# A hybrid decoder step: the prompt's recurrence in four 64-token chunks, laid two to a partition span

## The chip, the cores and the metric

The kernel runs on one core of a Trainium2 chip. The metric is the device time in microseconds (us) of one execution; the median of three runs is used. Engines are named as in the profile: PE is the tensor engine, DVE the vector engine, ACT the scalar engine, POOL GpSimd, SP the engine whose queue issues the DMAs.

## The reference

One layer of a hybrid decoder for a prompt of 256 tokens and 8 sequences of 8 new tokens each ("the sample", 64 tokens), width 2048. A combined input projection feeds a convolution group (31 taps) and an RWKV-7 group of 16 heads of 64; then come an output projection, cross-attention into 256 memory tokens and a gated ConvFFN. The change is in the RWKV-7 group, whose core is this recurrence over the tokens, per head, with a 64x64 state `S`:

```
def wkv_step(S, inp):
    r, w, k, v, a, b = inp
    sa = jnp.einsum('bhij,bhj->bhi', S, a)
    S = S * w[:, :, None, :] + sa[..., None] * b[:, :, None, :] + v[..., None] * k[:, :, None, :]
    y = jnp.einsum('bhij,bhj->bhi', S, r)
    return S, y
...
seq = tuple(jnp.moveaxis(z, 1, 0) for z in (rh, heads(decay), kh, vh, -kk, kk * ah))
S_new, ys = lax.scan(wkv_step, wkv.astype(f32), seq)
```

The prompt starts from a zero state, each sample sequence from its own given state; the states after the last token are outputs too.

## The kernel before

Weights stream from HBM in pieces of 1024 columns in three buffers (`wpiece`, L144 on): ACT writes the upper fp16 part `whi` (L153), DVE the rest `wlo` (L154), and each product of a weight tile takes three fp16 matmuls of 320 columns (`acc`, L56). Everything else is in fp32; in the trace each fp32 matmul stands as two records, a transpose and an fp16 matmul as one.

The order of PE is written out by hand. `drive` takes the weights' matmuls in groups of three, and between them `step` runs a piece of another stream whenever its time has come. A stream is a generator that yields how long its next piece should stay away, in us of a clock that `mm` and `turn` advance by the matmuls' columns. Streams are: `first_stage` (`prepare`, per pair of heads), two `second_stage` streams (`pair`, for the even and the odd pairs), the convolution's taps on DVE (`taps`, `cvmix`, L827 and L829) and its smaller pieces. So one piece of a stream stands on PE as a short run of fp32 matmuls, here called a burst, between the `acc` matmuls. There are 8 pairs of heads; a pair's 128 channels fill the partitions, 64 per head.

`prepare` makes the decayed operands of a pair: `AR` (removal key and receptance), `bt`, `kt`, their token-major copies `tvkb` (`tv`, `tk`, `tb`), and `pc`, the decay over a chunk. `pair` cuts the prompt into two chunks of 128 tokens and does this:

- Score products (`pA`): per chunk and head `bt` and `kt` (64 channels) times `AR`, 128x256 each; DVE masks them into `AB` (L610) and `AM` (L611). The sample has one 64x64 form of them (`AMs`, L618).
- `invert`: the inverse of a triangular 128x128 matrix for 2 chunks x 2 heads by doubling: levels 1 to 4 with 32-row blocks side by side (`psZ`, `psX`), level 5 on 32-blocks, level 6 on 64-blocks (`psZ<-TQ,AB`, `psG<-GG,zm`).
- `sample_state`: the sample's states are loaded as block-diagonal matrices `BD`, one per sequence, transposed (`pS`, 8 per pair) and multiplied with the operands (`pXR`). The decays are spread over the partitions by two fp16 matmuls (`pPC`), and DVE multiplies them with the states into `SD` (L658).
- `prompt_part`: per chunk `solve` makes `pX` (its result `x` copied by ACT), `pU` (`u`, copied by DVE, L684) and `pY`; then the state (`pSc`; `S`, L705, L721 and L722). All of these use the whole 128-row array.
- `sample_part`: its own small `invert`, `solve`, and the new states `pSn`, to which DVE adds `SD` (L754).

PE executes in this fixed order: a burst whose operand is late holds everything behind it.

Of the kernel before, what the change touches and what calls it, by code (L numbers as in the profile page):

```python
# [17 lines left out]
P = 128  # L18
# [27 lines left out]
def hybrid_step_kernel(ctx: ExitStack, tc: tile.TileContext, I, O):  # L46
# [34 lines left out]
    bones16 = cst.tile([P, P], F16, name="bones16")  # L81
    V.tensor_copy(bones16, bones)
# [6 lines left out]
    mask4 = cst.tile([P, 4, P], U8, name="mask4")  # L89
# [4 lines left out]
    RM = cst.tile([P, 330], F16, name="RM")  # L94
    V.memset(RM, 1.0)
    V.memset(RM[:, 0:258:129], 0.0)
    V.memset(RM[:, 258:330:9], 0.0)

# [3 lines left out]
    with tc.tile_pool(name="mk", bufs=1) as mk:  # L102
        f = mk.tile([P, P], F32, name="mkf")
        for ty in range(2):
            G.memset(f, 1.0)
            keep(f, [[1, P]], -1 + ty, -1)
            for z in (ty, ty + 2):
                V.tensor_copy(mask4[:, z, :], f)
# [202 lines left out]
    AMs_ = [ra.tile([P, 3, 4, P], F32, name=f"AM{q}") for q in range(2)]  # L311
    AMss_ = [ra.tile([64, 4, 2, 64], F32, name=f"AMs{q}") for q in range(2)]
    ABs_ = [ra.tile([P, 4, P], F32, name=f"AB{q}") for q in range(2)]
    BDs_ = [ra.tile([P, NB, P], F32, name=f"BD{q}") for q in range(1)]
    LGs_ = ra.tile([P, 330], F32, name="LG")
    GGp_ = [ra.tile([P, 4, P], F32, name=f"GG{q}") for q in range(2)]
    GGs_ = [ra.tile([64, 2, 64], F32, name=f"GGs{q}") for q in range(2)]
    ARS_ = [ra.tile([P, NB, 32], F32, name=f"ARS{q}") for q in range(2)]
    TQ_ = [ra.tile([64, 4, 64], F32, name=f"TQ{q}") for q in range(2)]
    cleared = AMs_ + AMss_  # L320
    for t_ in ABs_ + AMs_ + AMss_ + BDs_ + GGp_ + GGs_ + TQ_ + ARS_:
        (V if any(t_ is v_ for v_ in cleared) else G).memset(t_, 0.0)
# [23 lines left out]
    # d[256+9b+j] pairs pb[256+9b+j] with pb[257+9b+j]; token j of batch b sits at pb[257+9b+1+j]  # L346
# [19 lines left out]
    def invert(A_, GG, TQ, nm, C, nlev):  # L366
# [3 lines left out]
        blk = [slice(32 * q, 32 * q + 32) for q in range(nb)]  # L370
        Gc = rb.tile([C, nm, 32], F32, tag="Gc" + s, name="Gc")
# [3 lines left out]
        for q, r in enumerate(blk):  # L375
            V.copy_predicated(Gc[r, :, 1::2], EM[r, 16 * q:16 * q + 16].unsqueeze(1).broadcast_to([32, nm, 16]), A_[r, :, 32 * q + 1:32 * q + 32:2])
        V.transpose(Tf, Gf)
        yield 1.69
        for lev in range(1, min(nlev, 5)):
# [6 lines left out]
            for a in range(nm):  # L386
                for q, r in enumerate(blk):
                    mm(psZ[r, a * 16:(a + 1) * 16].rearrange("p (n m) -> p n m", m=m), A_[r, a, r], half(Tc, a, r), True, True, True)
# [11 lines left out]
        for q, r in enumerate(blk):  # L400
            (A.copy if q % 2 else G.tensor_copy)(GG[r, :, r], Gc[r])
        if nlev > 5:
            for r in blk[:2]:
                A.copy(TQ[r, :, r], Tc[r])
        for lev in range(5, nlev):
            m = 1 << lev
            first = [slice(2 * q * m, (2 * q + 1) * m) for q in range(C // (2 * m))]
            second = [slice((2 * q + 1) * m, (2 * q + 2) * m) for q in range(C // (2 * m))]
            Tl, Gl = ((lambda r, a: Tc[r, a, :]), (lambda r, a: Gc[r, a, :])) if m == 32 else ((lambda r, a: TQ[r, a, r]), (lambda r, a: GG[r, a, r]))
            psZ = mtile("psZ")  # L410
            for a in range(nm):
                for r1, r2 in zip(first, second):
                    mm(psZ[r2, a * m:(a + 1) * m], A_[r1, a, r2], Tl(r1, a), True, True, True)
            zm = rb.tile([C, nm * 64], F32, tag="zm" + s, name="zm")
            for q, r2 in enumerate(second):
                (V.tensor_copy if q else A.copy)(zm[r2, 0:nm * m], psZ[r2, 0:nm * m])
            yield 3.14
            psG = mtile("psG")
            for a in range(nm):
                for r1, r2 in zip(first, second):  # L420
                    if lev < nlev - 1 and r2.stop <= 64:
                        mm(psG[r2, a * m:(a + 1) * m], Gl(r2, a), zm[r2, a * m:(a + 1) * m], True, True, True)
                    mm(psG[r1, a * m:(a + 1) * m], zm[r2, a * m:(a + 1) * m], Gl(r2, a), True, True, True)
            pv = psG[:, 0:nm * m].rearrange("p (a m) -> p a m", m=m)
            for q, (r1, r2) in enumerate(zip(first, second)):
                if lev < nlev - 1 and r2.stop <= 64:
                    A.copy(TQ[r2, :, r1], pv[r2])
                (V.tensor_copy if q else A.copy)(GG[r1, :, r2], pv[r1])
# [45 lines left out]
    def pr(t_):  # L474
        return t_[:, 0:256].rearrange("p (c t) -> p c t", t=P)
# [10 lines left out]
    def prepare(i, r, k, v):  # L486
        c = slice(i, i + 1)
        # decay, a, gate from the low-rank projections
# [5 lines left out]
        def e_(name, w=T):  # L494
            return ra.tile([P, 330], F32, tag="e", bufs=5, name=name)[:, :w]
# [5 lines left out]
        A.activation(LGs_[:, 0:258].rearrange("p (c t) -> p c t", t=129)[:, :, 1:129], pr(pw), AF.Tanh, bias=hv[:, 0, c], scale=0.5)  # L501
        A.activation(LGs_[:, 258:330].rearrange("p (b e) -> p b e", e=9)[:, :, 1:9], sm(pw), AF.Tanh, bias=hv[:, 0, c], scale=0.5)
# [15 lines left out]
        # inclusive sums of log decay over each chunk  # L518
        L1 = e_("L1", 330)
        V.tensor_scalar(L1, LGs_, 1.0, None, ALU.add)  # L520
        V.tensor_tensor_scan(L1, RM, L1, 0.0, ALU.mult, ALU.add)
        LP = L1[:, 0:258].rearrange("p (c t) -> p c t", t=129)
        LS = L1[:, 258:330].rearrange("p (b e) -> p b e", e=9)
        mid = rb.tile([P, 2, 2], F32, tag="mid", name="mid")
        V.tensor_scalar(mid[:, 0, :], LP[:, :, 64], C1, None, ALU.mult)
        V.tensor_scalar(mid[:, 1, :], LP[:, :, 64], -C1, None, ALU.mult)
        PX = e_("PX", 330)
        PP = PX[:, 0:258].rearrange("p (c t) -> p c t", t=129)
        PS = PX[:, 258:330].rearrange("p (b e) -> p b e", e=9)
        IP = e_("IP")  # L530
        em = rb.tile([P, 2], F32, tag="em", name="em")
        pc = rb.tile([P, 10], F32, tag="pc", bufs=3, name="pc")
        for ch in range(2):
            A.activation(PP[:, ch, :], LP[:, ch, :], AF.Exp, bias=mid[:, 1, ch:ch + 1], scale=C1)
            A.activation(IP[:, ch * P:(ch + 1) * P], LP[:, ch, 1:129], AF.Exp, bias=mid[:, 0, ch:ch + 1], scale=-C1)
        A.activation(PS, LS, AF.Exp, scale=C1)
        A.activation(sm(IP), LS[:, :, 1:9], AF.Exp, scale=-C1)
        A.activation(em, mid[:, 0, :], AF.Exp)
# [1109 lines left out]
```

## Time and profile before

| what | value |
|---|---|
| timed runs | 2122.68, 2119.32, 2120.03 us; median 2120.03 us |
| the profiled execution | 2122.2 us from its first to its last instruction |
| PE busy | 2040.3 us (96%) |
| DVE busy | 1453.0 us (68%) |
| ACT busy | 982.1 us (46%) |
| POOL busy | 582.3 us (27%) |
| stage with the RWKV pairs | about 100 to 650 us of the span |

PE's records overlap, since matmuls are pipelined: a record's own duration is its latency. What a matmul costs PE is read in the time line from its start to the start of the next.

### The profile page before, as it was taken

Reading aid. Unit: us, or ns where it says so; the run is one execution under the profiler, and the core shown is the slowest. Engines: PE = TensorE matmul, PEld = TensorE weight load, DVE = VectorE, ACT = ScalarE, POOL = GpSimd, SP = SyncE. Lnnn points to the kernel's source line nnn. Section 1 sums busy time; section 2 is a strip of 40 time slices with the busy share of each in tenths; the row PEclk is TensorE's granted clock in tenths of the full one; section 3 lists DMA queues with packets and bytes.
Section 4 is the critical chain, followed back from the end, with each engine's and each line's share of the span. In section 5 each row is a group of like instructions: output and inputs, shape, how many; then the busy total and the mean of one; then the engine's idle time right before and its main releaser. Section 6 shows DMA issues by size and latency. Waiting matters only on the chain.

```text
span 2122.2 us, 43823 instructions
## 1 busy us (share of the span) xinstructions
PE 2040.3 (96%) x17221; PEld 1424.2 (67%) x17221; DVE 1453.0 (68%) x2772; ACT 982.1 (46%) x1686; POOL 582.3 (27%) x913
## 2 busy tenths in 40 slices
PE   8999999999899999989999989999999999999998
PEld 6766667576554467566667767777777777777776
DVE  6698798797985834967784497666666666443344
ACT  5434434334544643755673354444444444533332
POOL 4624525335210301210001143433333323000000
PEclk9999999899999999999999999999999999999999
DMA  7533233333246675757784535555555555445444
GB/s 182 159 91 99 73 103 89 82 107 81 91 155 203 216 238 167 244 186 250 246 268 142 169 105 168 161 165 162 159 163 166 159 160 164 141 158 164 156 147 140
DMA packets 301995, 333.26 MB, mean 157 GB/s; under 512 B 33882, under 2 KB 227237, under 8 KB 301764
## 3 DMA queue, kind: packets, MB, share of 16 engines
q1 hardware_dynamic: 301788, 330.46, 51.0%
q8 instruction: 135, 2.21, 0.4%
q14 instruction: 72, 0.59, 0.1%
HBM read 319.90 MB, written 11.22 MB: 156 GB/s over the span
## 4 chain that ended last, share of the span: by engine, by line
PE 74%; DVE 13%; DMA 6%; ACT 2%; issue 2%; POOL 1%; SPq 0%; DVEq 0%; POOLq 0%; ACTq 0%
PE acc L56 58%; PE acck L56 6%; DVE cvmix L829 3%; DVE wlo L154 3%; DMA rawkv<-in_cache_mem_v_dram 2%; PE pA L56 1%; PE pk L60 1%; PE pY L56 1%; DVE vl L1267 1%; DMA out_dram<-fo 1%; ACT whi L153 1%; DMA raw<-in_w_v_dram 1%; ACT vh L1266 1%; PE pos L56 1%; DVE xr L1148 1%
## 5 line engine op out<-in xcount | busy, mean ns | idle before, releaser
L56 PE MATMUL acc<-h,whi 128*128 128x320 f16 (+1 forms) x4736 | 981.3, 301 | 11.5 <-DVE h L1150 3.9
L154 DVE SCALAR_TENSOR_TENSOR wlo<-raw,whi 128x1024 f16<-128x1024 f32 (+1 forms) x512 | 631.3, 1235 | 462.4 <-ACT whi L153 453.6
L56 PEld LDWEIGHTS <-whi 128*128 128x128 f16 (+1 forms) x7080 | 685.9, 99 | 280.5 <-issue 21.8
L153 ACT ACTIVATE whi<-raw 128x1024 f16<-128x1024 f32 (+1 forms) x512 | 533.1, 1044 | 616.3 <-PE acc L56 517.8
L56 PE MATMUL acc<-h,wlo 128*128 128x320 f16 (+1 forms) x2368 | 702.2, 301 | 0.2 <-DVE wlo L154 0.2
L56 PEld LDWEIGHTS <-wlo 128*128 128x128 f16 (+1 forms) x3540 | 348.2, 98 | 142.9 <-issue 7.6
L56 PE MATMUL acc<-act,whi 128*128 128x320 f16 x1320 | 270.3, 299 | 0.0
L56 PE MATMUL acc<-act,wlo 128*128 128x320 f16 x660 | 196.4, 299 | 0.0
L829 DVE SCALAR_TENSOR_TENSOR cvmix<-GB,cdw,cvmix 128x256 f32<-128x256 f32 (+1 forms) x480 | 187.3, 428 | 0.9
L56 PE MATMUL acck<-whi,memo 128*128 128x512 f16 x512 | 151.4, 380 | 0.6 <-ACT memo L949 0.6
L1497 POOL COPY nF<-U 128x9 f32<-128x9 f32 x88 | 52.2, 593 | 307.7 <-DVE U L1496 299.3
L56 PEld LDWEIGHTS <-memo 128*128 128x128 f16 x768 | 73.2, 99 | 80.7 <-issue 2.0
L1494 POOL COPY U<-stF 128x16 f32<-128x16 f32 x88 | 124.5, 1420 | 0.9 <-ACT stF L1482 0.9
L1132 POOL TENSOR_TENSOR sums<-sums,bsq 128x320 f32<-128x320 f32 x33 | 37.9, 1147 | 241.3 <-ACT bsq L1126 239.7
L56 PE MATMUL acck<-wlo,memo 128*128 128x512 f16 x256 | 95.6, 379 | 1.5 <-DVE wlo L154 1.5
L1502 DVE SCALAR_TENSOR_TENSOR C<-U,fdw,C 128x336 f32<-128x336 f32 x176 | 91.3, 558 | 0.1
L1500 ACT ACTIVATE C<-U,fdw 128x336 f32<-128x336 f32 x88 | 55.8, 659 | 31.2 <-DVE U L1496 31.2
L1495 DVE TENSOR_TENSOR U<-acc,rs 128x256 f32<-128x256 f32 x88 | 36.8, 418 | 39.4 <-PE acc L56 39.3
L1267 DVE SCALAR_TENSOR_TENSOR vl<-rawkv,vh 128x1024 f16<-128x1024 f32 x31 | 37.2, 1223 | 31.9 <-ACT vh L1266 31.9
L56 PE MATMUL acc<-oopb,whi 128*128 128x320 f16 x256 | 53.7, 299 | 1.1 <-DVE oopb L190 1.0
L1218 POOL CAST qs<-qf 128x64 f16<-128x64 f32 x16 | 10.0, 626 | 162.5 <-ACT qf L1215 162.5
L56 PE MATMUL acc<-cvmix,whi 128*128 128x320 f16 x256 | 52.1, 299 | 1.5 <-ACT memo L949 1.5
(477 smaller groups left out, 2601.2 us busy)
## 6 DMA issues: line engine op xcount, KB each, us to landing
raw<-in_w_up_dram SPq DMA_DIRECT2D x352, 256.0 KB
raw<-in_w_down_dram SPq DMA_DIRECT2D x71, 512.0 KB
raw<-in_w_in_dram SPq DMA_DIRECT2D x52, 512.0 KB
raw<-in_w_in_dram SPq DMA_DIRECT2D x64, 256.0 KB
raw<-in_w_k_dram SPq DMA_DIRECT2D x32, 512.0 KB
raw<-in_w_v_dram SPq DMA_DIRECT2D x32, 512.0 KB
raw<-in_w_out_dram SPq DMA_DIRECT2D x32, 512.0 KB
rawkv<-in_cache_mem_k_dram SPq DMA_DIRECT2D x32, 512.0 KB
```

Of the source, the lines that this page charges most:

```text
L56: pe[0] = TE.matmul(out, lhsT=lhsT, rhs=rhs, start=start, stop=stop, skip_group_check=skip)
L60: pe[0] = TE.transpose(out, in_, idn)
L153: A.activation(hi[:, :n], raw[:, :n], AF.Copy, scale=SW)
L154: V.scalar_tensor_tensor(lo[:, :n], raw[:, :n], SW, hi[:, :n], ALU.mult, ALU.subtract)
L829: late(V.scalar_tensor_tensor(o_, i_(j), cdw[:, c, j:j + 1], o_, ALU.mult, ALU.add))
L1132: (V if f > 11 else G).tensor_tensor(ssum, ssum, sq, ALU.add)
L1267: V.scalar_tensor_tensor(vl, raw, SX, vh, ALU.mult, ALU.subtract)
L1494: G.tensor_copy(us[:, :, 0:2], stF[:, :, :, j])
L1495: V.tensor_tensor(U[:, 2:258], acc[:, 0:256], rf[:, 0:256], ALU.mult)
L1497: G.tensor_copy(nF[:, :, 0, j], U[:, 256:338:10])
L1500: A.activation(c, U[:, 0:336], AF.Identity, bias=fdw[:, 3, j:j + 1], scale=fdw[:, 0, j:j + 1])
L1502: V.scalar_tensor_tensor(c, U[:, t_:t_ + 336], fdw[:, t_, j:j + 1], c, ALU.mult, ALU.add)
```

## The change

The prompt is cut into four chunks of 64 tokens. Two neighbouring chunks share the partitions: the even one in 0 to 63, the odd one in 64 to 127 (`hcs`). A chunk's score products are 64x128, each on one quarter of the array (64 rows by the head, 64 columns by the chunk); four follow each other on the four quarters, the heads into different PSUM tiles. `AM` holds all four masked forms, so `AB` and its copy fall away. `invert` stops after level 5. The prompt's part runs through four chunks instead of two: products of 64x64 on quarters, one full-array product with the state `Sbd` per chunk after the first; `Z` and `Sbd` come from DVE, the chunk's own state `Ssc` and `Y` from ACT. The sample's states are loaded two to a tile (`N0`: 4 transposes per pair), `pXR` becomes 16 products of 32x64, `pPC` and `SD` fall away: 16 products with diagonal matrices `DP` (made by POOL) add the decayed states to `pSn` in PSUM. In `prepare`, `pn` is two transposes and a matmul. The last argument of `mm` tells the clock alone how many products are taken to run side by side.

```diff
-        for ch in range(2):
             for h in range(2):
-                rows = slice(64 * h, 64 * h + 64)
-                cols = slice(ch * P, (ch + 1) * P)
-                px = mtile("pA")
-                for z, s_ in enumerate((bt, kt)):
-                    mm(px[:, z * 256:(z + 1) * 256], s_[rows, cols], AR[rows, :, cols], True, True)
-                pxv = px.rearrange("p (y t) -> p y t", t=P)
-                V.copy_predicated(AB_[:, 2 * ch + h, :], mask4[:, 0], pxv[:, 0])
-                V.copy_predicated(AM[:, :, 2 * ch + h, :], mask4[:, 1:4], pxv[:, 1:4])
-                yield 0.53
+        for m in range(2):
+            pxs = [mtile("pA"), mtile("pA")]
+            for z, s_ in enumerate((bt, kt)):
+                for cp in range(2):
+                    ch = 2 * m + cp
+                    for h, hr in enumerate(hcs):
+                        mm(pxs[h][hcs[cp], z * P:(z + 1) * P], s_[hr, ch * 64:(ch + 1) * 64], AR[hr, ch * P:(ch + 1) * P], True, True, True, 4)
+            for h in range(2):
+                V.copy_predicated(AM[:, :, 2 * m + h, :], mask4, pxs[h][:, 0:256].rearrange("p (y t) -> p y t", t=64))
+            yield 0.6
...
+            pxr = [mtile("pXR"), mtile("pXR")]
             for z in range(2):
+                for j in range(4):
+                    b = 2 * j + z
+                    for h, hr in enumerate(hcs):
+                        mm(pxr[h][32 * j:32 * j + 32, 0:64], AF_[hr, 32 * b - 16 * z:32 * b - 16 * z + 32],
+                           S0T[hr, b % 4, hcs[b // 4]], z == 0, z == 1, True, 8)
...
-        inv_, sst_ = spawn(invert(AB_, GG, TQ, 4, P, 7)), spawn(sample_state())
-        _, (XT, SD) = yield from join(inv_, sst_)
+        inv_, sst_ = spawn(invert(AM, GG, 4, P, 6)), spawn(sample_state())
+        _, (XT, S0T, DP) = yield from join(inv_, sst_)
...
+            Sbd = Ssc = None
+            for ch in range(4):
+                m, cp = ch // 2, ch % 2
+                xr_, yr_ = hcs[cp], hcs[1 - cp]
+                px = mtile("pX")
+                for h, hc in enumerate(hcs):
+                    mm(px[xr_, hc], AM[xr_, 2 + cp, 2 * m + h, :], tv[xr_, m, hc], h == 0, False, True, 2)
+                    mm(px[yr_, hc], AM[xr_, 3 - cp, 2 * m + h, :], tv[xr_, m, hc], h == 0, False, True, 2)
+                if ch:
+                    mm(px[:, 0:P], AR[:, ch * P:(ch + 1) * P], Sbd, False, False, True)
+                x = rb.tile([P, P], F32, tag="x128", name="x")
+                A.activation(x[xr_], px[xr_, 0:P], AF.Copy)
+                yield 1.5
+                pu = mtile("pU")
+                for h, hc in enumerate(hcs):
+                    mm(pu[xr_, hc], GG[xr_, 2 * m + h, :], x[xr_, hc], True, True, True)
+                u = rb.tile([P, P], F32, tag="u128", name="u")
+                V.tensor_copy(u[xr_], pu[xr_, 0:P])
+                ps = mtile("pSc")
+                for hc in hcs:
+                    mm(ps[hc, 0:64], tk[xr_, m, hc], tv[xr_, m, hc], True, False, True, 2)
+                yield 1.1
+                for hc in hcs:
+                    mm(ps[hc, 0:64], tb[xr_, m, hc], u[xr_, hc], False, True, True, 2)
+                for h, hc in enumerate(hcs):
+                    mm(px[yr_, hc], AM[xr_, 1 - cp, 2 * m + h, :], u[xr_, hc], False, True, True)
+                Z = ps[:, 0:64]
+                if ch:
+                    Z = rb.tile([P, HD], F32, tag="Zs", name="Zs")
+                    V.tensor_tensor(Z, ps[:, 0:64], Ssc, ALU.add)
+                if ch < 3:
+                    Sbd = rb.tile([P, P], F32, tag="S1", name="S1")
+                    V.scalar_tensor_tensor(Sbd.rearrange("p (g f) -> p g f", f=HD), Z.unsqueeze(1).broadcast_to([P, 2, HD]), pc[:, ch:ch + 1],
+                                           bones.rearrange("p (g f) -> p g f", f=HD), ALU.mult, ALU.mult)
+                Ssc = rb.tile([P, HD], F32, tag="Ssc", name="Ssc")
+                A.activation(Ssc, Z, AF.Copy, scale=pc[:, ch:ch + 1])
+                A.activation(Y[yr_, m, :], px[yr_, 0:P], AF.Copy)
+                yield 1.5
...
+            for b in range(NB):
+                for hc in hcs:
+                    mm(px[hc, b * HD:(b + 1) * HD], S0T[hc, b % 4, hcs[b // 4]], DP[hc, b, :], False, b == NB - 1, True, 2)
+            SN = ra.tile([P, NB, HD], F32, tag="SN", name="SN")
+            A.activation(SN.rearrange("p b j -> p (b j)"), px, AF.Copy)
```

On PE, the score products of the first pair stood like this: four bursts for the prompt, of which the first is shown, and two for the sample, of which the first is shown (two rows make a burst; shapes are those of the output; `pss`, `pn` and `pa` belong to the next pair's `prepare`).

```order
L56 MATMUL pA<-AR,bt 128x256
L56 MATMUL pA<-AR,kt 128x256
L56 MATMUL pss<-bones,sq 128x2 x3
...
L56 MATMUL pn<-ident,rnx 128x128 x2
L56 MATMUL pn<-ident,rnx 128x64
L56 MATMUL pA<-AR,bt 64x128
L56 MATMUL pA<-AR,kt 64x128
```

Now they stand like this: two bursts for the prompt, of which the first is shown, and one for the sample.

```order
L56 MATMUL pA<-AR,bt 64x128 x4
L56 MATMUL pA<-AR,kt 64x128 x4
...
L56 MATMUL pss<-bones,sq 128x2 x3
...
L56 MATMUL pa<-lx_599,lw 128x320
L56 MATMUL pA<-AR,bt 64x128 x2
L56 MATMUL pA<-AR,kt 64x128 x2
```

Six bursts of the scores per pair have become three, with more and smaller products in each.

A chunk of 128 tokens of the recurrence stood on PE like this (the second chunk of a pair; the rows left out are `acc` rows and bursts of other streams).

```order
L56 MATMUL pX<-S_2678,AR 128x128
L56 MATMUL pX<-tvkb,AM_519 128x64 x2
...
L56 MATMUL pU<-x,GG_527 128x64 x2
...
L56 MATMUL pY<-S_2678,AR 128x128
L56 MATMUL pY<-u,AM_519 128x64
L56 MATMUL pY<-tvkb,AM_519 128x64
...
L56 MATMUL pSc<-tvkb 128x128
L56 MATMUL pSc<-u,tvkb 128x128
```

A chunk of 64 tokens now stands like this (the second of a pair).

```order
L56 MATMUL pX<-tvkb,AM_521 64x64 x4
L56 MATMUL pX<-S_2588,AR 128x128
...
L56 MATMUL pU<-x,GG_526 64x64 x2
L56 MATMUL pSc<-tvkb 64x64 x2
...
L56 MATMUL pSc<-u,tvkb 64x64 x2
L56 MATMUL pX<-u,AM_521 64x64 x2
```

The products of the recurrence shrank from 128 rows and columns of the array to 64x64, and stand in three bursts per chunk, of which there are four per pair.

## Rows read from the trace of the kernel before

**Rows 1.** The page's first part: the span; busy time, share, instructions of an engine.
```profile
span 2122.2 us, 43823 instructions
...
PE 2040.3 (96%) x17221; PEld 1424.2 (67%) x17221; DVE 1453.0 (68%) x2772; ACT 982.1 (46%) x1686; POOL 582.3 (27%) x913
```

**Rows 2.** Windows: from:to, length, busy time of each engine, granted clock, DMA.
```profile
100.00:650.00 550.00, 518.54 (x5852) 351.18 (x5849) 482.33 (x1255) 226.31 (x524) 207.13 (x296) 0.97 0.36 100
```

**Rows 3.** Waits of PE from 100 to 650 us: total us, times, longest.
```profile
PE psX L56 <- DVE zc L390: 4.7, 5, 1.8
PE pY L56 <- DVE u L684: 2.7, 2, 1.7
```

**Rows 4.** Time line of PE, a score burst of the prompt: start, length, records merged.
```profile
235.91 0.70 PE L56 MATMUL pA<-AR,bt 64*128 64x256 f32 x2
...
236.97 0.27 PE L56 MATMUL pss<-bones,sq 128*128 128x2 f32 x1
```

**Rows 5.** Time line of PE, a score burst of the sample.
```profile
246.28 0.43 PE L56 MATMUL pA<-AR,bt 64*64 64x128 f32 x2
...
246.85 0.45 PE L56 MATMUL acc<-h,whi 128*128 128x320 f16 x2
```

**Rows 6.** Time line of PE, a level of the inverse on four 32-row tiles.
```profile
128.87 0.44 PE L56 MATMUL psZ<-Tc,AB 32*32 32x16 f32 x32 [1.03 <-DVE Tc L377]
129.24 0.31 PE L56 MATMUL acc<-h,whi 128*128 128x320 f16 x1
```

**Rows 7.** Time line of PE, the sample's u on two column tiles.
```profile
482.15 0.45 PE L56 MATMUL pU<-x,GGs 64*64 64x64 f32 x8
482.54 0.45 PE L56 MATMUL acc<-h,whi 128*128 128x320 f16 x2
```

**Rows 8.** Time line of PE, the level on 64-row blocks.
```profile
480.12 0.44 PE L56 MATMUL acc<-h,whi 128*128 128x320 f16 x2
480.40 0.30 PE L56 MATMUL acc<-h,wlo 128*128 128x320 f16 x1
480.63 0.68 PE L56 MATMUL psG<-GG,zm 64*64 64x64 f32 x8
481.24 0.45 PE L56 MATMUL acc<-h,whi 128*128 128x320 f16 x2
```

**Rows 9.** Time line of PE, a burst of the prompt's recurrence on the whole array.
```profile
471.85 0.38 PE L56 MATMUL pY<-S,AR 128*128 128x128 f32 x2
472.07 0.33 PE L56 MATMUL pY<-u,AM 128*128 128x64 f32 x2
...
472.91 0.43 PE L56 MATMUL acc<-h,whi 128*128 128x320 f16 x2
```

**Rows 10.** Time line of PE, a transposition of sample states and a product with them.
```profile
125.46 0.60 PE L60 MATMUL pS<-ident,BD 128*128 128x128 f32 x4
125.90 0.44 PE L56 MATMUL acc<-h,whi 128*128 128x320 f16 x2
...
132.04 0.63 PE L56 MATMUL pXR<-S0T,ARS 128*32 128x128 f32 x8
132.73 0.81 PE L56 MATMUL pbon<-k,bones 128*128 128x320 f32 x2
```

**Rows 11.** Groups by line and shape, 100 to 650 us: count, busy us, mean ns, idle before.
```profile
L611 DVE COPY_PREDICATED AM<-mask,pA 128x384 f32<-128x384 uint8 x32 | 18.5, 577 | 0.0
L658 DVE SCALAR_TENSOR_TENSOR SD<-BD,pPC 64x512 f32<-64x512 f32 x16 | 10.9, 680 | 0.2
L610 DVE COPY_PREDICATED AB<-mask,pA 128x128 f32<-128x128 uint8 x32 | 9.3, 292 | 9.2 <-PE pA L56 8.8
L618 DVE COPY_PREDICATED AMs<-mask4s,pA 64x256 f32<-64x256 uint8 x16 | 6.8, 426 | 1.5 <-PE pA L56 1.4
```

**Rows 12.** Windows around the slowest stretch of the clock, columns as in Rows 2.
```profile
380.00:385.00 5.00, 4.01 (x22) 2.49 (x21) 3.84 (x5) 2.79 (x8) 3.60 (x4) 0.97 0.57 167
385.00:405.00 20.00, 20.00 (x65) 11.86 (x65) 14.38 (x45) 4.03 (x12) 5.82 (x8) 0.50 0.07 21
```

More of the change, by code (lines that the diff above doesn't have):

```diff
@@ L88, in hybrid_step_kernel @@
     V.memset(nhalf, -0.5)
-    mask4 = cst.tile([P, 4, P], U8, name="mask4")
+    mask4 = cst.tile([P, 4, 64], U8, name="mask4")
     mask4s = cst.tile([64, 4, 64], U8, name="mask4s")
@@ L370, in invert, with Ar @@
         blk = [slice(32 * q, 32 * q + 32) for q in range(nb)]
+        at = [32 * (q % 2) for q in range(nb)]
+        def Ar(q):
+            return A_[blk[q], q // 2 if C == P else 0]
         Gc = rb.tile([C, nm, 32], F32, tag="Gc" + s, name="Gc")
@@ L400, in invert @@
         for q, r in enumerate(blk):
-            (A.copy if q % 2 else G.tensor_copy)(GG[r, :, r], Gc[r])
+            (A.copy if q % 2 else G.tensor_copy)(GG[r, :, at[q]:at[q] + 32], Gc[r])
         if nlev > 5:
[L403 to L409, printed above, removed]
             psZ = mtile("psZ")
             for a in range(nm):
[L412 to L416, printed above, removed]
+                for q in range(0, nb, 2):
+                    mm(psZ[blk[q + 1], a * 32:(a + 1) * 32], Ar(q)[:, a, 32:64], Tc[blk[q], a, :], True, True, True)
+            zm = rb.tile([C, nm * 32], F32, tag="zm" + s, name="zm")
+            for q in range(0, nb, 2):
+                (V.tensor_copy if q else A.copy)(zm[blk[q + 1]], psZ[blk[q + 1], 0:nm * 32])
             yield 3.14
@@ L419, in invert @@
             for a in range(nm):
[L420 to L428, printed above, removed]
+                for q in range(0, nb, 2):
+                    mm(psG[blk[q], a * 32:(a + 1) * 32], zm[blk[q + 1], a * 32:(a + 1) * 32], Gc[blk[q + 1], a, :], True, True, True)
+            pv = psG[:, 0:nm * 32].rearrange("p (a m) -> p a m", m=32)
+            for q in range(0, nb, 2):
+                (V.tensor_copy if q else A.copy)(GG[blk[q], :, 32:64], pv[blk[q]])
             yield 1.31
@@ L494, in e_ @@
         def e_(name, w=T):
-            return ra.tile([P, 330], F32, tag="e", bufs=5, name=name)[:, :w]
+            return ra.tile([P, 332], F32, tag="e", bufs=5, name=name)[:, :w]
         sq = e_("sq")
@@ L646, in sample_state @@
-            PCd = ra.tile([P, 2, NB, HD], F16, tag="S0T", name="PCd")
-            pcs = rb.tile([P, 2, NB], F16, tag="pcs", name="pcs")
-            split(pcs[:, 0], pcs[:, 1], pc[:, 2:10], 1024.0)
-            for z in range(2):
-                G.tensor_tensor(PCd[:, z], pcs[:, z].unsqueeze(2).broadcast_to([P, NB, HD]), dsel16.unsqueeze(1).broadcast_to([P, NB, HD]), ALU.mult)
-            yield 1.89
-            px = mtile("pPC")
-            for z in range(2):
-                mm(px, bones16, PCd[:, z].rearrange("p b j -> p (b j)"), z == 0, z == 1)
@@ L655, in sample_state @@
-            SD = rb.tile([P, NB, HD], F32, tag="SD", name="SD")
+            DP = rb.tile([P, NB, HD], F32, tag="DP", name="DP")
+            G.tensor_tensor(DP, pc[:, 4:12].unsqueeze(2).broadcast_to([P, NB, HD]), dsel16.unsqueeze(1).broadcast_to([P, NB, HD]), ALU.mult)
+            S0T = rb.tile([P, 4, P], F32, tag="S0T", name="S0T")
+            px = mtile("pS")
+            for b4 in range(4):
+                turn(px[:, b4 * P:(b4 + 1) * P], N0[:, b4, :], ident)
+            A.activation(S0T.rearrange("p b f -> p (b f)"), px, AF.Copy)
```

259 lines of the change are left out of this document (104 added, 155 removed).

## The prediction

> **What bounds the kernel now.** The page gives PE 96% of the span [rows 1]. The change touches only the stage with the RWKV pairs, so the next view is the windows: from 100 to 650 us PE is busy 518.5 of 550 us and DVE 482.3 [rows 2]. So PE idles 31.5 us there, and DVE is 88% full. The waits of PE name small sums, nearly all for DVE: 4.7 us for `zc`, 2.7 us for `u` [rows 3]. PE therefore sets the pace, and DVE follows closely: what a burst costs PE should show in the time almost in full, as long as operands arrive. Those costs are read from the time line, from one start to the next; every burst is issued 8 times, once per pair, or a multiple of that.
>
> **Prices on PE.** On the whole array a record of 128 columns costs 0.11 us: the two of `pY<-S` take 471.85 to 472.07. A record of only 64 columns is hardly cheaper, eight take 472.07 to 472.91, 0.105 each [rows 9]. On one 64x64 tile, eight records of 64 columns take 0.61 us. But such a burst has a toll at both ends: the `acc` record ahead of it takes 0.23 to the next start, where the two before take 0.14 each [rows 8]. The way out is not resolved by these rows; I take 0.09 there as well, and an estimated 0.06 for the first product and the first `acc` behind: **0.24 us for each burst on part of the array that stands alone**, 0.12 per change. Then a record on one tile costs (0.61 - 0.14) / 8 = 0.058 us for 64 columns, and from [rows 5], (0.57 - 0.15) / 4 = 0.105 for 128. On two column tiles side by side eight records take 0.39 [rows 7], so a pair of records costs 0.06. On four tiles that share neither rows nor columns 32 records take 0.37 [rows 6]: less than 0.01 each, so tiles in different rows run side by side as well, even into one PSUM tile. Two tiles in the same columns and different rows stand nowhere in this trace; the new scores need them.
>
> The Trainium skill (TensorEngine Tiling (Array Packing), "Gotcha 1: PSUM Pressure") says that different row tiles cannot access the same PSUM bank at once; by that the new diagonal products, which write one bank from both row halves, would take turns. [Rows 6] speak against it; what it would cost is a rival below.
>
> **The change part by part, on PE.**
> 1. Prompt scores. Before: 32 bursts of 0.09 + 1.06 us [rows 4] = 36.8. After: 16 bursts of 16 records of 128 columns on four quarters, 4 x 0.11 + 0.24 = 0.68, sum 10.9. Change **-25.9**. If the row halves take turns: 8 x 0.11 + 0.24 = 1.12, sum 17.9, change -18.9. I take four, since [rows 6] is the nearest row.
> 2. Sample scores. Before 16 bursts of 0.09 + 0.57 [rows 5] = 10.6; after 8 of 8 records on two row halves, 0.68 = 5.4. **-5.2** (taking turns: 1.12, -1.6).
> 3. Sample states. Half of 16 runs of four transposes at 0.44 [rows 10] goes: **-3.5**. `pXR`: 16 bursts of 0.09 + 0.63 [rows 10], without a wait of 0.06 = 11.5 become 8 of 32 records on eight tiles, 4 x 0.058 + 0.24 = 0.47, sum 3.8: **-7.7** (taking turns -5.9). The 16 `pPC` matmuls of 512 columns at 0.22 (0.14 for 320 columns [rows 8]) go: **-3.5**.
> 4. New diagonal products: 32 records per pair on two tiles, 16 x 0.058 + 0.1 = 1.03: **+8.2** (taking turns +15.6).
> 5. Level 6 of the inverse goes: two bursts of 0.09 + 0.61 per pair [rows 8]: **-11.2**.
> 6. Recurrence. Before, 40 records of 0.107 and four of 0.11 per pair [rows 9]: 4.72, sum 37.8, and no toll, since all of it is on the whole array. After, per chunk: `pX` 8 records on two column tiles 0.23, `pU` 4 on one tile 0.23, `pSc` 2 x 0.12, the `u` part of `pX` 0.23, together 0.93; three bursts at 0.24; in three chunks of four a state product of 0.22. That is 4 x 1.65 + 0.66 = 7.26 per pair, sum 58.1: **+20.3**. In the new order some of these bursts stand next to other part-array bursts. Counting all changes of the tile shape along PE's order gives 71 more than before, where bursts standing alone would give 96 (48 bursts more on balance: 96 in the recurrence against 16, 8, 8 and 16 fewer in points 1, 2, 3 and 5). 25 x 0.12 comes back: **-3.0**.
> 7. `pn`: 16 of 48 full-array records go: **-1.8**.
>
> Sum -33.3 us. With row halves that take turns everywhere it is -13.5.
>
> **The other engines.** DVE loses the 64 masked copies of `AB` and `AM` (27.8 us) for 32 of 128x256, which at the nearest row, `AMs` with as many columns, are 13.6; and `SD`, 10.9 [rows 11]. Added to each other with the smaller edits (the sum into `SN`, two halves of `SPR` and the `pcs` go; `u`, `Z`, `Sbd` and a subtraction in `prepare` come) DVE's work shrinks by an estimated 25 to 30 us of 482, in about the proportion of PE's or a little better. ACT takes about as much as it gives, and POOL gets one product with the diagonal in place of two; at 226 and 207 busy of 550 [rows 2] both cover that. DMA moves the same bytes, and `N0` is free after its transposes, where `BD` was held until `SD`: a gain that I count at nothing.
>
> **New waits.** The chain inside a pair is longer: four rounds of `x`, `u` and state where there were two. PE waited 2.7 us for `u` in 24 rounds [rows 3] (two per pair for the prompt, one for the sample): 0.11 each, so 16 more give 1.8. The 24 states now pass two DVE instructions in a row, `Z` and `Sbd`, 1.5 of the clock's us before the next chunk; I price them at twice a wait for `zc` (4.7 us in 48 levels, 0.1 each [rows 3]), 4.8. Behind a late state stand the next chunk's `pX` and all `acc` after it. Together **+6.6**; at least 0, and at 0.5 us for each of the 40 added rounds 20.
>
> **Sum.** -33.3 + 6.6 = -26.7 us. The profiled span of 2122.2 lies 2.2 above the median and within the runs, so I take the change from the median: 2120.0 - 26.7 = **2093 us**.
>
> **The rivals.**
> - *Row halves take turns* everywhere: -13.5 + 6.6, 2113 us. For it: no row shows two tiles in the same columns. Against: [rows 6].
> - *Only the diagonal products take turns*, for their common bank, as in the skill's rule above: 7.4 less is gained, 2101 us. [Rows 6] has that form on smaller tiles.
> - *More than the sum*: DVE's relief takes 10 of the 31.5 us of idle time, and the half-clock stretch goes. From 385 to 405 us the granted clock is 0.50, its lower level of 1.2 GHz, after five us in which PE was busy for 4.0 [rows 12]; that costs about 10. With both, 2073 us. For it: the idle time that went ahead of the stretch is one of waits for slower engines. Against: new waits can cause such a stretch as well.
> - *The chain of the recurrence sets the end* (the other side): with DVE 88% full, a `u` or `Sbd` stands behind a weight piece or masked copies in DVE's queue, and PE waits in each added round. From 33.3 / 40 = 0.83 us a round on, nothing is left; at 1.0 us, 2127 us. For it: the longest wait for `u` was 1.7 us; against it: only two waits for `u` in 24 rounds.
> - *No change*: what PE saves comes back as waits for DVE's weight pieces and taps, 2120 us. Against it: DVE's own work falls as well.
>
> **How the numbers follow.** A measurement of this kernel can tell about 0.2%, 4.2 us, from no change. Chances: my sum 0.50, row halves 0.13, diagonal alone 0.10, more than the sum 0.11, no change 0.07, the chain 0.09. The first four are faster by more than 4.2 us: 0.84; same 0.07; slower 0.09. The range goes from 2076, short of the case with more gain, to 2115, past both cases of turns; most of the likeliest case (2087 to 2102, with waits from 0 to 15) lies inside.
>
> **What would show it.** A prompt score burst of 16 `pA` records should take 0.5 to 0.6 us from its first start to the next `acc` (1.0 if halves take turns). The diagonal run of `pSn` should take some 0.95 us. Busy time of DVE in the stage should fall by 25 us or more, and the stage end about 27 us sooner. PE's waits for `u` and `S` should stay below 10 us together. The prediction fails if the 64x64 products of the recurrence cost more than 0.06 a pair, if the toll is larger between two part-array shapes, or if a new stretch at half clock appears.

## The result and the profile after

The changed kernel takes 2106.36 us (median of 4 runs, 2104.2 to 2106.68), the kernel before 2121.36 us on the same chip: ratio 0.9933, interval 0.9917 to 0.995, some 15 us faster. The forecast was 26.7 us, 2093. The sign was right and the time lies in the forecast range; the size is a bit over half.

The page after, its first part (the columns of [rows 1]):

```profile
span 2102.5 us, 45190 instructions
...
PE 2014.7 (96%) x17941; PEld 1395.5 (66%) x17941; DVE 1430.7 (68%) x2727; ACT 985.4 (47%) x1702; POOL 583.0 (28%) x908
```

PE's busy time fell by 25.6 us. Windows of the changed kernel: the stretch of [rows 2], then a wait at 207 us and what follows it:

```profile
100.00:650.00 550.00, 507.44 (x6654) 328.92 (x6651) 471.31 (x1218) 237.48 (x553) 196.58 (x301) 0.97 0.38 105
...
205.00:210.00 5.00, 3.96 (x61) 2.94 (x55) 4.88 (x13) 1.33 (x5) 2.68 (x5) 1.00 0.47 129
210.00:213.40 3.40, 3.40 (x36) 2.18 (x37) 3.37 (x9) 1.37 (x5) 2.34 (x4) 0.50 0.00 0
213.40:218.00 4.60, 4.60 (x47) 3.04 (x43) 4.60 (x9) 2.02 (x6) 4.26 (x8) 1.00 0.40 85
```

The wait itself, in the time line of PE:

```profile
208.10 0.33 PE L56 MATMUL pSc<-u,tvkb 64*64 64x64 f32 x4 [1.04 <-DVE u L678]
```

In the same 550 us PE now idles 42.6 us instead of 31.5. After the wait of 1.04 us the granted clock stands at 0.50 (1.2 GHz) for 3.4 us, in which PE is busy all the time at half speed: wait and slow stretch together cost about 2.7 us. Not every wait of this size brings such a stretch (last section). Who is waited for, PE from 100 to 650 us (as [rows 3]):

```profile
PE px L60 <- DVE bon L566: 7.2, 5, 2.3
PE psZ L56 <- DVE Tc L399: 6.8, 3, 3.8
PE pSc L56 <- DVE u L678: 6.1, 5, 2.2
PE psZ L56 <- DVE Tc L379: 2.7, 2, 1.4
PE psZ L56 <- DVE zc L392: 2.4, 1, 2.4
PE pX L56 <- DVE S L693: 2.3, 4, 1.2
```

The time line of PE, a prompt score burst (as [rows 4]) with the recurrence's products behind it:

```profile
236.08 0.45 PE L56 MATMUL pA<-AR,bt 64*64 64x128 f32 x8
236.35 0.40 PE L56 MATMUL pA<-AR,kt 64*64 64x128 f32 x8
236.56 0.29 PE L56 MATMUL pSc<-u,tvkb 64*64 64x64 f32 x4
236.69 0.39 PE L56 MATMUL pX<-u,AM 64*64 64x64 f32 x4
```

Sixteen records take 0.48 us from the first start to the next burst; where an `acc` follows, as the forecast had it (0.5 to 0.6), they take 0.60. DVE's groups that answer to [rows 11]:

```profile
L610 DVE COPY_PREDICATED AM<-mask,pA 128x256 f32<-128x256 uint8 x32 | 12.3, 436 | 6.7 <-PE pA L56 6.7
L678 DVE COPY u<-pU 64x128 f32<-64x128 f32 x32 | 9.0, 283 | 9.1 <-PE pU L56 8.8
L617 DVE COPY_PREDICATED AMs<-mask4s,pA 64x256 f32<-64x256 uint8 x16 | 6.3, 429 | 0.1
L693 DVE SCALAR_TENSOR_TENSOR S<-Zs,pc,bones 128x128 f32<-128x128 f32 x16 | 6.0, 375 | 0.2
L690 DVE TENSOR_TENSOR Zs<-pSc,Ssc 128x64 f32<-128x64 f32 x24 | 5.2, 219 | 5.3 <-PE pSc L56 4.8
```

**Where the time went.** I cut both traces from the first product of `prepare` (`pw`) to the first product of the output projection, and added up PE's records there: the time in which PE works, the time in which it waits, and, from the clock's rows, how much of the work ran at half clock. Half of the latter is the clock's loss; work without it is the work at full clock.

```
                        length   work at full clock   clock's loss   PE waits   DVE busy
before                   648.9        599.1               15.1         34.7       548.2
changed                  632.8        568.2               18.2         46.4       528.6
old_chunks_scores_merged 650.7        575.7               18.2         56.8       548.9
..._scores_and_states    649.3        572.9               20.0         56.4       533.0
before_u_by_scalar       643.6        599.1               12.7         31.8       546.0
scores_half_by_half      635.7        567.7               18.5         49.6       528.0
before_short_taps        629.7        598.2                3.4         28.0       501.3
changed_short_taps       623.1        567.0               17.6         38.5       482.4
u_by_scalar_engine       625.0        567.9               17.0         40.1       518.5
u_scalar_dead_copy       630.2        567.2               17.5         45.4       529.3
scores_twice             641.2        575.1               15.7         50.4       529.4
state_by_scalar_engine   626.8        575.0               10.2         41.6       512.1
u_scalar_taps_spaced     632.0        566.5               18.3         47.2       522.5
```

The work fell by 30.9 us, where the prices had said 33.3. Of it 11.7 came back as waits and 3.1 as lost clock, so the cut is 16.1 shorter; the rest of the program is 3.6 us shorter. The profiled spans differ by 19.7 us, the medians by 15.0: single executions of one kernel differ by several us (23 runs of the kernel before on one chip went from 2117 to 2127), so a few us of one profile prove nothing. Behind the cut all these kernels run the same work, and yet their profiles take from 1380.0 to 1387.7 us there.

### The profile page after: what moved, and what is told of

It is laid out like the page before. It is cut to its first block, busy times and chain, and to the rows that moved or that the text cites. A ratio compares the mean times of both kernels' runs of the same rounds, so it can differ in the third digit from the quotient of the medians.

```text
span 2102.5 us, 45190 instructions
## 1 busy us (share of the span) xinstructions
PE 2014.7 (96%) x17941; PEld 1395.5 (66%) x17941; DVE 1430.7 (68%) x2727; ACT 985.4 (47%) x1702; POOL 583.0 (28%) x908
## 4 chain that ended last, share of the span: by engine, by line
PE 72%; DVE 14%; DMA 6%; ACT 3%; issue 2%; POOL 2%; SPq 0%; DVEq 0%; POOLq 0%; ACTq 0%
PE acc L56 57%; PE acck L56 6%; DVE wlo L154 3%; DVE cvmix L820 3%; DMA rawkv<-in_cache_mem_v_dram 3%; DVE vl L1258 1%; PE pX L56 1%; DMA rawkv<-out_dram 1%; DMA out_dram<-fo 1%; ACT whi L153 1%; PE pk L60 1%; ACT vh L1257 1%; DVE xr L1139 1%; PE pSn L56 0%; PE pU L56 0%
## 5 line engine op out<-in xcount | busy, mean ns | idle before, releaser
L56 PEld LDWEIGHTS <-whi 128*128 128x128 f16 (+1 forms) x7080 | 687.0, 99 | 278.1 <-issue 15.3
L820 DVE SCALAR_TENSOR_TENSOR cvmix<-GB,cdw,cvmix 128x256 f32<-128x256 f32 (+1 forms) x480 | 181.9, 418 | 0.8
L1485 POOL COPY U<-stF 128x16 f32<-128x16 f32 x88 | 128.8, 1469 | 0.9 <-ACT stF L1473 0.7
L1491 ACT ACTIVATE C<-U,fdw 128x336 f32<-128x336 f32 x88 | 55.8, 659 | 30.9 <-DVE U L1487 30.9
```

The source lines that it names most:

```text
L56: pe[0] = TE.matmul(out, lhsT=lhsT, rhs=rhs, start=start, stop=stop, skip_group_check=skip)
L820: late(V.scalar_tensor_tensor(o_, i_(j), cdw[:, c, j:j + 1], o_, ALU.mult, ALU.add))
L1485: G.tensor_copy(us[:, :, 0:2], stF[:, :, :, j])
L1491: A.activation(c, U[:, 0:336], AF.Identity, bias=fdw[:, 3, j:j + 1], scale=fdw[:, 0, j:j + 1])
```

## The experiments

The theory from these profiles: PE's saving is real, but DVE gives it back, since its queue runs full in stretches and what PE waits for stands in it behind other streams' work. The rivals: PE alone sets the pace, and some price was wrong; or the longer chain of the recurrence eats the gain.

**1. The order of the quarters.** The head's loop stands outside, so all four products on one row half are issued ahead of the four on the other (two records each).

```diff
-            for z, s_ in enumerate((bt, kt)):
-                for cp in range(2):
-                    ch = 2 * m + cp
-                    for h, hr in enumerate(hcs):
+            for h, hr in enumerate(hcs):
+                for z, s_ in enumerate((bt, kt)):
+                    for cp in range(2):
+                        ch = 2 * m + cp
```

> The changed kernel, with the score products of the prompt issued head by head, so that only two quarters of the array (one row half) are in use at a time. My account (four quarters run side by side and PE's time counts in full): a burst goes from 0.49 to about 0.93 us from its first record to the next start, 16 bursts, 7 us slower than the changed kernel, so about 2113 us. Rival (PE has slack behind DVE, so a longer burst is hidden): the burst is longer all the same, but the time rises by less than 2 us.

Measured: 2107.64 us, ratio 0.9935 (0.9918 to 0.9953), as the changed kernel. The burst did not grow, so the run tells nothing on what 0.4 us more of PE cost. It tells something else: the eight `bt` records of one burst still start within 0.19 us (239.184 to 239.377), and all `kt` records after them, though the program issues the first head's `kt` products ahead of the second head's `bt`:

```profile
239.18 0.46 PE L56 MATMUL pA<-AR,bt 64*64 64x128 f32 x8
239.45 0.41 PE L56 MATMUL pA<-AR,kt 64*64 64x128 f32 x8
```

PE had started products on a free tile ahead of earlier ones whose tile was busy. So the fixed order of PE is that of issue; on parts of the array, single products can start out of it.

**2. PE's saving alone.** The kernel before, in its old chunks, with both heads' score products in one burst, for the prompt and the sample. The pause behind a burst comes once where it came twice, so the clock of the streams changes as well.

```diff
+            pxs = [mtile("pA"), mtile("pA")]
+            for z, s_ in enumerate((bt, kt)):
+                for h, hr in enumerate(hcs):
+                    mm(pxs[h][:, z * 256:(z + 1) * 256], s_[hr, cols], AR[hr, :, cols], True, True, False, 2)
             for h in range(2):
...
-                px = mtile("pA")
-                for z, s_ in enumerate((bt, kt)):
-                    mm(px[:, z * 256:(z + 1) * 256], s_[rows, cols], AR[rows, :, cols], True, True)
```

> The kernel before (two chunks of 128, recurrence on the whole array) with one edit: both heads' score products in one burst, alternating between the row halves and into two PSUM tiles. My account (row halves run side by side, and the recurrence on quarters costs about as much as the rest of the change gains): 16 bursts of 4 x 0.216 + 0.24 = 1.1 us in place of 32 of 1.15, 19 us, and 5 for the sample's; 24 us faster than before, 2097 us, so faster than the changed kernel too. Rival (only quarters run side by side, or the gain of the change comes from the shorter inverse and the sample's states): at most 6 us faster than before, 2115 us or more.

Measured: 2125.41 us, ratio 1.0019 (1.0007 to 1.0031). Its time line of PE (the first two rows) and of DVE:

```profile
235.84 0.70 PE L56 MATMUL pA<-AR,bt 64*128 64x256 f32 x4
236.37 0.60 PE L56 MATMUL pA<-AR,kt 64*128 64x256 f32 x4
236.90 0.83 PE L56 MATMUL pss<-bones,sq 128*128 128x2 f32 x6
...
122.80 0.43 DVE L619 COPY_PREDICATED AMs<-mask4s,pA 64x256 f32<-64x256 uint8 x1
123.13 0.83 DVE L521 TENSOR_TENSOR_SCAN L<-RM,L 128x330 f32<-128x330 f16 x1
123.89 0.41 DVE L619 COPY_PREDICATED AMs<-mask4s,pA 64x256 f32<-64x256 uint8 x1
124.20 1.21 DVE L154 SCALAR_TENSOR_TENSOR wlo<-raw,whi 128x1024 f16<-128x1024 f32 x1
125.33 0.72 DVE L830 SCALAR_TENSOR_TENSOR cvmix<-GB,cdw,cvmix 128x256 f32<-128x256 f32 x2
125.98 0.29 DVE L377 STREAM_TRANSPOSE Tc<-Gc 128x128 f32<-128x128 f32 x1
...
126.42 0.58 PE L56 MATMUL psZ<-Tc,AB 32*32 32x16 f32 x32 [3.47 <-DVE mid L526]
```

Two heads' products take 1.06 us where one head's took 1.06 before [rows 4]: the row halves run side by side. PE's work fell by 23.4 us, and 22.1 came back as waits, 3.1 as clock. The lower rows show how: PE stands still for 3.47 us from 122.95 on, until `psZ` starts, which needs `Tc` (the profile puts the end of the wait down to `mid`, which DVE runs just behind `Tc`). In that time DVE runs a masked copy, a scan and another masked copy, a weight piece of 1.21 us and two taps, and only then the transposition that makes `Tc`. The Trainium skill (TensorE: Matmul & The Clock Gate, "Architectural detail") says that DVE takes its instructions strictly in order; these rows agree.

**3. The old chunks with the new sample states** as well (`N0`, `pXR` on eight tiles, the diagonal products; no `pPC`, no `SD`):

```diff
-            SD = rb.tile([P, NB, HD], F32, tag="SD", name="SD")
...
+            DP = rb.tile([P, NB, HD], F32, tag="DP", name="DP")
+            G.tensor_tensor(DP, pc[:, 2:10].unsqueeze(2).broadcast_to([P, NB, HD]), dsel16.unsqueeze(1).broadcast_to([P, NB, HD]), ALU.mult)
```

> The kernel of old_chunks_scores_merged with the change's part for the sample's states added (states loaded two to a tile, products on eighths of the array, decayed states added by diagonal products, no pPC and no SD). My account by PE's prices: 3.5 + 7.7 + 3.5 gained and 8.2 lost, 6.5 us, and DVE loses 17 us of work, which takes some of PE's waits: 7 to 12 us faster than old_chunks_scores_merged, about 2088 us. Rival (the diagonal products eat what the states gain): within 3 us of it.

Measured: 2123.42 us, ratio 1.0005 (0.9994 to 1.0017), 2 us below the merged scores alone, where the rival had said within 3. PE's work fell by 2.8 us, not by 6.5. DVE has 15.2 us less to do than before, and still nothing is gained: PE waits 56.4 us. DVE's load alone does not foretell the time either.

**4. `u` copied by ACT**, in the changed kernel, and the same edit in the kernel before.

```diff
-                V.tensor_copy(u[xr_], pu[xr_, 0:P])
+                A.activation(u[xr_], pu[xr_, 0:P], AF.Copy)
```

> The changed kernel, with the prompt's u copied from PSUM by ACT in place of DVE. My account (PE's waits for u come from DVE's queue): the waits of PE for u, 7.1 us in the stage, fall under 2 us, and the kernel is 4 to 7 us faster, about 2101 us. Rival (the waits follow DVE's total load and only change their name): PE's idle time in the stage stays within 3 us of 46, and the time within 2 us of the changed kernel's.

> The kernel before, its prompt's u copied by ACT in place of DVE: 16 copies of 0.284 us, 4.5 us of DVE's work. Theory A: 4 to 8 us faster than before, as the same edit gave 10 us with 32 copies in the changed kernel. Theory C (the edit helped there because the four-round recurrence waits for u, and here are only two rounds): 0 to 3 us.

Measured: in the changed kernel 2095.86 us, ratio 0.9879 (0.9864 to 0.9895), 10 us faster by an edit that takes 9 us of work from DVE and leaves PE's work as it was; that is more than the 4 to 7 expected. In the cut it is 7.8 us. In the kernel before 2118.42, ratio 0.9985 (0.9969 to 1.0001): 4.5 us of work moved, 3 us gained, at the edge of what can be told; theory C had said 0 to 3. PE's waits after, in the changed kernel with `u` by ACT:

```profile
PE px L60 <- DVE bon L566: 8.3, 4, 2.7
PE pX L56 <- DVE S L693: 5.4, 5, 1.6
PE psZ L56 <- DVE Tc L399: 3.8, 1, 3.8
```

The wait for DVE's `u` is gone (1.6 us of waits for ACT's `u` are left), that for `S`, the next link, has grown from 2.3 to 5.4 us.

**5. Load or chain?** Again `u` by ACT, but DVE's 32 copies stay where they were, into a tile that nobody reads.

```diff
+                dead = rb.tile([P, P], F32, tag="dead", bufs=1, name="dead")
+                V.tensor_copy(dead[xr_], pu[xr_, 0:P])
```

> The changed kernel with the prompt's u copied by ACT, and the same 32 copies by DVE kept as dead work at the same places, into a tile that nobody reads. DVE's load is that of the changed kernel (about 9 us more than in u_by_scalar_engine), but the link of the recurrence's chain through DVE is gone. Theory L (the 10 us came from DVE's load): 2104 to 2108 us. Theory K (they came from taking a link of the chain out of DVE's queue, where it waits behind taps and weight pieces): 2094 to 2099 us, as u_by_scalar_engine.

Measured: 2103.59 us, ratio 0.9914 (0.9901 to 0.9928), just under the 2104 to 2108 of theory L. Most of the gain is gone, 7.7 of 10.5 us, with no reader for these copies. Their group:

```profile
L680 DVE COPY dead<-pU 64x128 f32<-64x128 f32 x32 | 9.1, 284 | 4.5 <-ACT u L678 4.1
```

So 9.1 us of DVE's work, at places where PE waits for DVE, cost 7.7 us by the medians; in the cut it was 5.2, with 5.3 more of waits, and the rest of the two profiles' difference lies outside the cut, where both run the same work. The row also shows that DVE stood still for 4.1 us ahead of these copies until ACT had written `u`: what was added is work and standing in the queue together. The link of the chain itself was worth about 3 us, which is not clear of the noise: the interval of this run overlaps the changed kernel's.

**6. DVE relieved elsewhere.** Taps of 64 columns in place of 256 from the second tap on, in three kernels. This leaves out three quarters of the prompt's convolution.

```diff
+                    if o_.shape[1] == 256:
+                        o_, i_ = cv[:, 0:64], lambda j: GB[:, j:j + 64]
```

> The kernel before, with the taps of the convolution's prompt part cut from 256 columns to 64 from the second tap on (three quarters of the prompt's convolution are left out); instructions and PE's order through the stage are the same. In the trace before, such a tap takes 517 ns with 256 columns and 340 with 64, so some 240 x 0.18 = 43 us of DVE's work go. Theory A (DVE's queue sets the pace together with PE, and PE waits behind taps for weight pieces and operands): faster, 2085 to 2105 us, PE's idle time between the first product of prepare and the second phase's end falls from 34.7 us to below 20. Theory B (PE alone sets the pace): within 5 us of 2120. This run is above all the base for the next two.

> The old chunks with both heads' score products in one burst (24.6 us less PE work than before, but no gain in time), again with the short taps. Theory A: with DVE relieved, what PE saves counts: 12 to 25 us below before_short_taps. Theory B' (what swallowed the saving was not DVE's queue but the streams' own pacing or ACT and POOL): within 5 us of before_short_taps, as with full taps.

> The changed kernel with the short taps. Theory A: 20 to 33 us below before_short_taps, nearer to the -26.7 us of the prediction's sum than the -15 us measured with full taps. Theory B': about 15 us below, as with full taps.

Measured: 2107.4 us, ratio 0.9942 (0.9921 to 0.9962), for the kernel before; 2103.95, 0.9909 (0.9885 to 0.9934), with merged scores; 2094.6, 0.9882 (0.9858 to 0.9905), for the changed kernel. (The second has no row in the table.) The first lies just above theory A's 2085 to 2105 and well below theory B's; PE's waits fell from 34.7 to 28.0, not below 20. Of the merged scores' 23 us some 7 now count by the ratios and 3.5 by the medians, and the intervals overlap: nearer to theory B' (within 5) than to the 12 to 25 of theory A. The change is worth 12.8 us here, about the 15 of theory B', not the 20 to 33 of theory A. The table shows that PE's work fell by 31 again, and that 10.5 came back as waits and 14.2 as clock, of which the kernel before lost only 3.4; but these two profiles differ by 2.3 us where the medians differ by 12.8, so the split is that of two executions and not a typical one. A full queue of taps is not the whole story.

**7. More work for PE**: the changed kernel issues each prompt score product twice. In the clock of the streams each counts for half, so that the clock stays as it was.

```diff
-            for z, s_ in enumerate((bt, kt)):
+            for z, s_ in enumerate((bt, kt, bt, kt)):
```

> The changed kernel, its prompt score products issued twice (the second time over the first, the same values): 16 bursts of 32 records in place of 16, each some 0.44 us longer, 7 us more PE work at places that the recurrence does not wait for, with the clock of the streams unchanged. If PE alone sets the pace: 7 us slower than the changed kernel, 2112 to 2115 us. If PE's work at these places is covered by waits that follow: within 3 us of it, 2103 to 2109.

Measured: 2113.88 us, ratio 0.9971 (0.9959 to 0.9983), 7.5 us slower than the changed kernel. Its burst:

```profile
238.18 0.45 PE L56 MATMUL pA<-AR,bt 64*64 64x128 f32 x8
238.44 0.40 PE L56 MATMUL pA<-AR,kt 64*64 64x128 f32 x8
238.66 0.40 PE L56 MATMUL pA<-AR,bt 64*64 64x128 f32 x8
238.88 0.40 PE L56 MATMUL pA<-AR,kt 64*64 64x128 f32 x8
239.10 0.29 PE L56 MATMUL pSc<-u,tvkb 64*64 64x64 f32 x4
```

The second half takes 0.44 us, 16 times: 7.0 us, and the time shows them in full. In the cut it is 6.9 us of work, 4.0 more of waits and 2.5 less of clock's loss. So PE does set the pace at these places; of the changed kernel's 15.3 us of score products, 9.7 lie in slices of time in which DVE is not full (below).

**8. Two tries to go on from `u` by ACT**: the chunk's state by a product with the identity and two copies by ACT; and the taps further apart.

```diff
+                if ch:
+                    mm(ps[:, 0:64], ident, Ssc, False, False, True)
...
-                    V.tensor_tensor(Z, ps[:, 0:64], Ssc, ALU.add)
...
+                    for hc in hcs:
+                        A.activation(Sbd[hc, hc], ps[hc, 0:64], AF.Copy, scale=pc[hc, ch:ch + 1])
```

> u_by_scalar_engine, and in addition the chunk's state without DVE: the earlier state is added in PSUM by one more product with the identity (24 of 128x64), and ACT writes the two diagonal blocks of Sbd from PSUM (48 copies of 64x64). DVE loses 24 x 0.22 and 24 x 0.36 = 13.9 us, ACT gets some 48 x 0.27 = 13, PE some 24 x 0.11 and tolls, 3 to 6. Theory K: the other link of the recurrence's chain goes, 2083 to 2092 us, PE's wait for S (5.4 us after the first edit) gone. Theory L, at the rate of the short taps (43 us of DVE for 12 us of time), about 4 us less PE's 3 to 6: 2094 to 2099 us.

```diff
-                    yield 1.18
+                    yield 1.35
```

> u_by_scalar_engine with the taps further apart (1.35 us of the clock from pair to pair of taps in place of 1.18), so that DVE's queue holds fewer taps while a pair's inverse runs, and more of them later. Theory L (a queue that is full in stretches): 3 to 10 us faster than u_by_scalar_engine, 2086 to 2093 us. Theory K: the chain's links still stand behind one tap each, so within 3 us, 2093 to 2099 us; slower if the taps' end then becomes late.

Measured: 2105.85 us, ratio 0.9929 (0.9916 to 0.9943), and 2108.16, ratio 0.994 (0.9927 to 0.9952). Both lie some 7 us or more above what either theory gave. The state's wait is no longer among PE's, but the 24 products cost PE 7.1 us, 0.30 each: a product is two records, and my expectation had counted one. The cut is 1.8 us longer than with `u` alone, and another 8.1 us are lost outside it, 7.5 of them behind it, where both kernels run the same work; why, stays open. With the taps apart, PE's waits for `bon`, `k` and `Tc` come to 19.1 us, and the waits in the cut rose by 7.1 in all. In the slices of 5 us of the next section DVE is full (at 97% or more) in 175 us here, against 230 with `u` alone: less of a full DVE did not mean less waiting. The last tap now ends at 650.4 us, 9.3 behind the last product of the last pair, where it ended at 620.9, 16.6 ahead of it; theory K had named that case as one that is slower. The best version run is `u` by ACT alone, 2095.86 us.

## Why the prediction was right in sign and too large

**The prices held in their sum**, 30.9 us against 33.3, with single terms that were off and partly cancelled. In us of PE's work at full clock, each record taken from its start to the next start: scores 28.0 less (31.1 forecast for points 1 and 2 together), `pXR` 5.3 (7.7), `pS` 3.7 (3.5), `pPC` 3.7 (3.5), the inverse's `psG` and `psZ` 9.5 (11.2), `pn` 1.8 (1.8); the recurrence cost 9.0 in the records of `pX`, `pU`, `pY` and `pSc` and 3.8 in the `acc` and `acck` that stand behind bursts, together 12.8 (20.3 less 3.0); the diagonal products 8.6 (8.2).

**The account of the shortfall.** In the cut 16.1 us were gained and 26.7 forecast. Of the 10.6 that are missing, 2.4 is work of PE that did not fall, 5.1 is waits beyond the 6.6 that were priced, and 3.1 is clock, which the sum had at nothing. These are differences of single profiles: `scores_half_by_half`, with the same products as the changed kernel in another order, has 3.2 us more of waits.

**The rivals of the prices fell.** Tiles in the same columns and different rows run side by side (1.06 us for two heads' products, experiment 2), so *row halves take turns* is out. The diagonal products of a pair (32 records) take 1.08 us in seven of the eight pairs, 34 ns a record, where one tile alone was priced at 58 (the forecast was some 0.95 us):

```profile
250.29 1.15 PE L56 MATMUL pSn<-DP,S0T 64*64 64x64 f32 x32
251.36 0.81 PE L56 MATMUL pg<-lx,gw 128*128 128x320 f32 x2
```

So the two row halves write one bank, each its own partitions of it, without taking turns. The Trainium skill (TensorEngine Tiling (Array Packing), "Gotcha 1: PSUM Pressure") says that different row tiles cannot access the same bank at once; these rows, on different partitions of one bank, show no turns. *More than the sum* fell too: stretches at half clock in the cut went from four to ten, one of the four being of 20.5 us, and the clock's loss rose from 15.1 to 18.2.

**The waits that were priced came as priced only in their sum**: `u` and `S` from 2.7 to 9.4 us, 6.7 more against 6.6. The parts are the other way round: `u` rose by 4.4 where 1.8 was priced, and `S` came to 2.3 where 4.8 was. That the sum agrees is luck. *The chain sets the end* would have needed five times as much.

**The step that failed** is the reading of the bound: "PE therefore sets the pace, and DVE follows closely: what a burst costs PE should show in the time almost in full, as long as operands arrive". The condition was priced for `u` and `S` alone. An average of 88% for DVE hid two kinds of stretches. Two windows of the kernel before, of 25 us (columns as [rows 2]):

```profile
125.00:150.00 25.00, 22.04 (x263) 14.40 (x261) 24.82 (x64) 7.77 (x16) 7.17 (x8) 1.00 0.29 79
325.00:350.00 25.00, 24.99 (x225) 18.78 (x223) 23.48 (x63) 8.67 (x20) 11.50 (x19) 1.00 0.38 101
```

In the first DVE is full and PE idles 3 us; in the second PE is full, with DVE at 94%. In slices of 5 us from the first `pw` to the last product of the last pair (570 us), DVE is at 97% or more in 305 us, and 23.1 of PE's 31.5 us of waits lie there; so do 25.8 of the 46.8 us of score products. What is saved on PE there should only make it wait sooner; this is argued and not shown, and one count speaks against it as the whole cause: with merged scores, of the 22.2 us of added waits only 1.1 lie in such slices. That PE waits sooner for a busy DVE is the mechanism of the rival *no change*, "what PE saves comes back as waits for DVE's weight pieces and taps", which got 0.07: for merged scores alone it came true in full (experiment 2), for the whole change in part, 5.0 us of waits for others than `u` and `S` and 3.1 us of clock. During PE's waits of over 0.3 us in the changed kernel (44.3 us), DVE was executing for 43.1 of them, 23.7 on taps and weight pieces.

Against it the prediction had set that "DVE's own work falls as well". It did, and experiments 4 and 5 show that this counts, 7.7 us of time for 9.1 of work; but it fell by 19.6 us in the cut, not by 25 to 30. The estimate had named `u`, `Z` and `Sbd` among what comes without a number for them; the prompt's `u` is 4.5 us more than before, and `Zs` and `S` together 6.1.

That the time lies in the range is in part luck too. It lies outside the 2087 to 2102 of the likeliest case; the range reached to 2115 for the cases of turns, which did not come.

What stays open: why a DVE relieved by 15 us (experiment 3) or by 47 (experiment 6) gave so little, while 9 us at `u` gave 10. About half of the merged scores' saving lay in full slices, but nearly all of the added waits lie in slices in which DVE is not full, where a short backlog, as in the rows at 123 us, is enough. Where each one falls seems to depend on how taps, weight pieces and pairs happen to meet, and every edit moves that: the misses of experiment 8 have the size of the gain of experiment 4. Only experiment 7 changed PE's work with the clock of the streams as it was, and it added work; no run took work away in this manner, so the streams' own pacing stays a rival that is not tested.

## What to carry to other kernels

Read a second engine that is 85 to 90% busy by windows and not by its mean, and price a saving on the first engine with the waits it may turn into: here 23 us of PE's work gave nothing, while 7 us of added work cost its price. Time of the second engine at places where the first one waits for it is worth more than its time elsewhere: moving 9 us of copies to an engine that was 43% busy gave 10 us, while 47 us of shorter taps gave 14. A wait of PE can be paid again in clock: in the cut of the changed kernel 46.4 us of waits went with 18.2 us of clock's loss.

## What was not expected of the hardware

- PE starts products on a free tile ahead of earlier ones of the program whose tile is busy: in experiment 1 eight `bt` records started within 0.19 us, although four `kt` records stood between them in the program (239.18 and 239.45 us in its rows).
- The granted clock fell to 0.50 for 3.4 us or more after waits that were this short: each of the ten such stretches in the cut of the changed kernel has a wait of 1.0 to 3.8 us shortly ahead of it, in three cases still running at its start. The reverse does not hold: of 19 waits of over 1 us there, eight have no such stretch in the 7 us behind them, and of 14 in the kernel before, twelve have none, the longest of them 2.1 us.
- Work added to PE cost its full price (7.0 us of work, 7.5 of time), work taken from it at the same kind of place nothing (23.4 us of work, no time), in two kernels that PE's busy share of 96% does not tell apart.
